# FFN gate and up by token, with seven block products in place of eight for three of eight pairs

## The chip, the core and the metric

One NeuronCore of a Trainium2 chip runs the whole program. Its engines work side by side, each through its own list of instructions: PE (matmul; the profile's PEld is its weight load), DVE (VectorE), ACT (ScalarE), POOL (GpSimd), and SP, which issues most transfers. The metric is the device time of one execution in microseconds, lower is better; the kernel before has a median of 2854.82 us in 3 runs (2853.4 to 2855.13).

## What is computed

One decoder layer on x of 256 tokens and width 2048, in float32: a SwiGLU FFN, a mixer (attention and a state space branch), and a second FFN. The change lies in the two FFNs:

```python
def rms_norm(x, g, eps=RMS_EPS):
    y = xf * lax.rsqrt(jnp.mean(xf * xf, axis=-1, keepdims=True) + eps)
    return (y * g.astype(jnp.float32)).astype(x.dtype)

def swiglu(x, w_gate, w_up, w_down):
    return (jax.nn.silu(x @ w_gate) * (x @ w_up)) @ w_down
...
f = swiglu(rms_norm(h, ffn1_pre_g[i]), ffn1_w_gate[i], ffn1_w_up[i], ffn1_w_down[i])
h = h + 0.5 * rms_norm(f, ffn1_post_g[i])
```

The hidden width is 5632. `w_gate` and `w_up` are 2048 x 5632, `w_down` is 5632 x 2048.

## The kernel before

**Precision.** Each product of two float32 matrices is made of three products of parts: every operand is split into hi (rounded by a copy on ACT) and lo (the rest, a subtraction on DVE), and hi*hi, hi*lo and lo*hi are summed in PSUM. For weights that is `split` (lines 99 to 113): `w_hi` on ACT at L111, `w_lo` on DVE at L112, for 1024 elements of each partition at a time. The pool `wsplit` has 4 buffers of each, so that a split is made when PE has done with the fourth before it. The operand that stays (x, or the hidden values) is split once into a `slot`.

**Weights stream.** Every slab of 1 MB comes through one of three buffers `raw`, by a transfer on SP (L131, L151), and is used once.

**Two forms of projection.** `project` (L121) works by token: x is the operand that PE holds, 128 tokens at a time, and 512 columns of weights move: three matmuls of 512 columns for each 128 rows of weights and each of two token blocks (L117 to L119). `project_t` (L164) works by channel: PE holds 128 x 128 of the weights, and the tokens move, hi and lo of all 256 tokens as 512 columns against `w_hi` (L159), hi alone as 256 columns against `w_lo` (L161). One `project_t` takes 256 output columns through 16 blocks of 128 rows; its result has channels on the partitions.

**FFN.** `ffn` (L290) takes 11 slabs of 512 hidden columns in groups of 4, 4 and 3. For a slab it calls `project_t` four times, gate and up for each half; POOL multiplies gate with the inverse norm of each token before and after the sigmoid function of ACT (L305, L307), DVE multiplies with up (L310), and `fill` splits the result into a slot as it is. After a group, `project` adds the group's part of the down projection to `f`. The norm's factor is spread over partitions once (`spread`), since channels lie on the partitions here.

**Order.** The program is recorded in the order of the code and then put, engine by engine, into an order that the framework's scheduler finds; an engine works through its list strictly. `pre_slots` and `PostNorm` stand between the stages. x and the residual h lie in two buffers of 1 MB (`hpool`).

Of the kernel before, what the change touches and what calls it, by code (L numbers as in the profile page):

```python
# [41 lines left out]
def decoder_layer(ctx: ExitStack, tc: tile.TileContext, x, x_t, cols, rows, post_g, wg1, wu1, wd1, w_in,  # L43
                  w_in_t, w_dt, w_att, w_ssm, w_out, wg2, wu2, wd2, out):
# [10 lines left out]
    acc = E(name="acc", bufs=2, space=bass.MemoryType.PSUM)  # L55
    psm = E(name="psm", bufs=4, space=bass.MemoryType.PSUM)
# [90 lines left out]
    def chunk_t(ps, xs, w, n, c, raw=None, before=None):
        parts = 2 if raw and c == 0 else 1
        if not raw:
            raw = raws.tile([P, 8, 256], F32, name="raw")  # L150
            loaded[0] = nc.sync.dma_start(raw, w(n, c))  # L151
        for b in range(2 * c, 2 * c + 2):
# [614 lines left out]
```

## Time and profile before

| what | value |
|---|---|
| median of 3 runs | 2854.82 us |
| profiled execution, its own time | 2855.79 us |
| its span, first to last instruction | 2853.7 us |
| PE busy | 2814.1 us, 99% |
| DVE busy | 1707.1 us, 60% |
| ACT busy | 1375.2 us, 48% |
| POOL busy | 283.1 us, 10% |
| DMA, mean | 188 GB/s |

The span is cut into stages by their windows: FFN 1 from 7 to 743 us, the mixer to 2103, FFN 2 to 2843. In a row of groups the first number behind the bar is the time in which any of the group was busy, the second the mean of one in ns, and then comes the idle time of its engine just before them, with what ended it. Matmuls overlap, so the time from one start to the next tells their pace.

### The profile page before, as it was taken

What the parts mean: (1) busy time and instruction counts of PE and PEld (TensorE: products, weight loads), DVE (VectorE), ACT (ScalarE), POOL (GpSimd) and SP (SyncE); (2) the same over time, 40 slices, a digit from 0 to 9 for tenths busy, and PEclk for the clock granted to TensorE, in tenths of its full rate; (3) what the DMA queues carried; (4) which work ended last, traced back from release to release, by engine and by line L of the source; (5) the groups of instructions that cost most, each with busy time, mean ns of one, the idle gap of its engine ahead of it and who ended that gap; (6) DMA issues with size and microseconds to landing.
All of it is one profiled execution on the core that took longest, in us unless ns stands there. A gap on an engine that the chain in (4) does not pass through costs nothing.

```text
span 2853.7 us, 36114 instructions
## 1 busy us (share of the span) xinstructions
PE 2814.1 (99%) x14540; PEld 2392.7 (84%) x14540; DVE 1707.1 (60%) x2018; ACT 1375.2 (48%) x1695; POOL 283.1 (10%) x219
## 2 busy tenths in 40 slices
PE   8999999999999999999999999999999999999998
PEld 7888888888788888888788888888878888888887
DVE  6554555555678766777765555545565545555555
ACT  5444444444555555545444444444455444443443
POOL 1100110011013110112100000000001100110110
PEclk9999999999999999999999999999999999999999
DMA  6565555556554555545555545555545555555554
GB/s 240 192 220 190 191 186 190 193 188 205 192 193 168 185 177 176 194 163 192 206 178 176 172 169 183 198 195 187 195 165 189 191 192 192 185 186 195 190 197 155
DMA packets 77127, 537.44 MB, mean 188 GB/s; under 512 B 8672, under 2 KB 8816, under 8 KB 13728
## 3 DMA queue, kind: packets, MB, share of 16 engines
q1 hardware_dynamic: 73152, 521.17, 53.1%
q0 software_dynamic: 3664, 13.80, 1.5%
q8 instruction: 114, 1.87, 0.2%
q14 instruction: 53, 0.43, 0.0%
q10 hardware_dynamic: 144, 0.17, 0.0%
HBM read 530.84 MB, written 4.26 MB: 188 GB/s over the span
## 4 chain that ended last, share of the span: by engine, by line
PE 91%; issue 4%; DVE 3%; ACT 0%; DMA 0%; POOL 0%; SPq 0%; DVEq 0%; POOLq 0%; ACTq 0%
PE acc L159 32%; PE acc L161 16%; PE acc L118 13%; PE acc L119 13%; PE acc L117 13%; DVE w_lo L112 1%; PE pyd L526 1%; PE tp L206 1%; DVE dec L506 1%; PE sc L619 0%; PE po L647 0%; DMA xT<-in_x_t 0%; PE pyo L538 0%; PE pst L533 0%; PE acc_t L119 0%
## 5 line engine op out<-in xcount | busy, mean ns | idle before, releaser
L112 DVE TENSOR_TENSOR w_lo<-raw,w_hi 128x1024 fp32r<-128x1024 f32 (+1 forms) x979 | 1243.9, 1274 | 1026.2 <-ACT w_hi L111 1020.1
L111 ACT ACTIVATE w_hi<-raw 128x1024 fp32r<-128x1024 f32 (+1 forms) x979 | 1034.5, 1059 | 1242.7 <-PE acc L159 619.6
L159 PE MATMUL acc<-slot,w_hi 128*128 128x512 f32 x4096 | 1295.6, 398 | 8.8 <-DVE slot L194 6.9
L161 PEld LDWEIGHTS acc<-slot,w_lo 128*128 128x128 f32 x4096 | 770.1, 188 | 187.8 <-DVE w_lo L112 6.4
L161 PE MATMUL acc<-slot,w_lo 128*128 128x256 f32 x4096 | 807.1, 278 | 4.2 <-DVE w_lo L112 4.2
L118 PE MATMUL acc<-w_lo,slot 128*128 128x512 f32 x1776 | 693.9, 391 | 5.5 <-DVE w_lo L112 5.5
L117 PE MATMUL acc<-w_hi,slot 128*128 128x512 f32 x1776 | 698.0, 393 | 0.0
L119 PE MATMUL acc<-w_hi,slot 128*128 128x512 f32 x1776 | 693.4, 390 | 0.0
L159 PEld LDWEIGHTS acc<-slot,w_hi 128*128 128x128 f32 x4096 | 626.9, 189 | 12.5 <-ACT w_hi L111 9.5
L118 PEld LDWEIGHTS acc<-w_lo,slot 128*128 128x128 f32 x1776 | 334.6, 188 | 76.8 <-DVE w_lo L112 6.5
L117 PEld LDWEIGHTS acc<-w_hi,slot 128*128 128x128 f32 x1776 | 334.6, 188 | 70.3 <-issue 1.2
L119 PEld LDWEIGHTS acc<-w_hi,slot 128*128 128x128 f32 x1776 | 334.4, 188 | 69.3
L305 POOL TENSOR_TENSOR pt<-pt,rb 128x512 f32<-128x512 f32 x44 | 59.9, 1361 | 1110.3 <-DVE pt L177 1105.2
L177 DVE TENSOR_TENSOR pt<-acc,pt 128x512 f32<-128x512 f32 x128 | 87.3, 682 | 1.3 <-ACT pt L176 1.3
L176 ACT ACTIVATE pt<-acc 128x512 f32<-128x512 f32 x128 | 74.3, 580 | 1.2 <-PE acc L161 1.2
L307 POOL TENSOR_TENSOR pt<-pt,rb 128x512 f32<-128x512 f32 x44 | 65.5, 1488 | 32.8 <-ACT pt L306 32.8
L481 DVE SCALAR_TENSOR_TENSOR xc<-pt,col,xc 128x255 f32<-128x255 f32 (+2 forms) x144 | 60.7, 475 | 12.0 <-ACT xc L478 11.9
L513 POOL TENSOR_TENSOR dec<-dec,cb 128x1024 f32<-128x1024 f32 x16 | 54.1, 3394 | 117.7 <-ACT dec L508 117.7
L387 POOL TENSOR_TENSOR pt<-pt,rb 128x512 f32<-128x512 f32 x24 | 34.7, 1447 | 215.7 <-DVE pt L177 154.8
L478 ACT ACTIVATE xc<-pt,col 128x256 f32<-128x256 f32 x48 | 26.9, 595 | 33.8 <-POOL pt L387 33.7
L306 ACT ACTIVATE pt<-pt 128x512 f32<-128x512 f32 x44 | 27.8, 632 | 28.7 <-POOL pt L305 28.7
L310 DVE TENSOR_TENSOR pt<-pt 128x512 f32<-128x512 f32 x44 | 30.5, 692 | 8.8 <-POOL pt L307 4.4
(195 smaller groups left out, 1036.5 us busy)
## 6 DMA issues: line engine op xcount, KB each, us to landing
raw<-in_wu SPq DMA_DIRECT2D x88, 1024.0 KB, 4.9
raw<-in_wd SPq DMA_DIRECT2D x88, 1024.0 KB, 4.9
raw<-in_wg SPq DMA_DIRECT2D x87, 1024.0 KB, 4.9
raw<-in_w_in SPq DMA_DIRECT2D x80, 1024.0 KB, 4.9
raw<-in_w_in_t SPq DMA_DIRECT2D x80, 1024.0 KB, 4.9
raw<-in_w_ssm SPq DMA_DIRECT2D x32, 1024.0 KB, 4.9
raw<-in_w_att SPq DMA_DIRECT2D x16, 1024.0 KB, 4.9
raw<-in_w_out SPq DMA_DIRECT2D x16, 1024.0 KB, 5.0
```

The lines of the kernel that those rows point to most:

```text
L111: nc.scalar.activation(hi[:, js], raw[:, js], AF.Copy)
L112: nc.vector.tensor_tensor(out=lo[:, js], in0=raw[:, js], in1=hi[:, js].bitcast(F32), op=ALU.subtract)
L117: nc.tensor.matmul(ps, xh, wh, start=first, stop=False)
L118: nc.tensor.matmul(ps, xh, wl, start=False, stop=False)
L119: nc.tensor.matmul(ps, xl, wh, start=False, stop=last)
L159: nc.tensor.matmul(ps[:, f], hi[:, j, wf[f]], sl[:, j], start=b + j == 0, stop=False)
L161: nc.tensor.matmul(ps[:, f, TT:], lo[:, j, wf[f]], sl[:, j, :TT], start=False, stop=b == len(xs) - 1 and j == 3)
L176: nc.scalar.activation(out[-1], p[:, :, TT:], AF.Copy)
L177: nc.vector.tensor_tensor(out=out[-1], in0=p[:, :, :TT], in1=out[-1], op=ALU.add)
L305: nc.gpsimd.tensor_tensor(out=g, in0=g, in1=rb, op=ALU.mult)
L307: nc.gpsimd.tensor_tensor(out=g, in0=g, in1=rb, op=ALU.mult)
L481: nc.vector.scalar_tensor_tensor(out=xc[:, j, d:], in0=v[:, k, :TT - d], scalar=w(3 - d), in1=xc[:, j, d:], op0=ALU.mult, op1=ALU.add)
```

## The change

Gate and up go by token, in slabs of 512 hidden columns (11 for each FFN), over 8 pairs of 128-row blocks of the inner width. A transfer of 1 MB now brings a pair's four blocks: gate and up of two row blocks. For five pairs, 8 block products (two token blocks x two row blocks x gate and up) are 24 matmuls. For pairs 2, 4 and 6 (`SP`) seven products take their place, on sums of x's blocks (`sums`, made once in an FFN) and on sums of the weights, which POOL makes from each slab with four additions (`wsum`, L351 to L354) before they are split like weights. Four of the seven (`p1`, `p5`, `p6`, `p7`) have PSUM banks of their own, and are combined on DVE and ACT after the last of the three pairs (L378 to L383); the ordinary pairs are summed in four banks. All 8 banks are then one pool, which the mixer's projections use as well.

The result has tokens on the partitions: the inverse norm becomes a scale for each partition (L390, L392) and POOL has no product there any more, but PE must transpose each slab's result (8 transposes, `to_slot`) before the down projection. Groups are 3, 3, 3 and 2 slabs. The weight sums use the two buffers of `hpool`, so x is read into them late (by POOL's queue, before the last down projection), and the residual of the mixer is written to memory first (`hsave2`).

```diff
+NP = D // (2 * P)
+SP = (2, 4, 6)
+ORDER0 = tuple(range(NP))
+ORDER = (2, 0, 4, 1, 6, 3, 5, 7)
...
-    acc = E(name="acc", bufs=2, space=bass.MemoryType.PSUM)
-    psm = E(name="psm", bufs=4, space=bass.MemoryType.PSUM)
+    psm = E(name="psm", bufs=8, space=bass.MemoryType.PSUM)
...
+            xf = tmp.tile([P, 8, P], F32, name="xf", tag="xc", bufs=2)
+            for f, t, k in ((0, 0, 0), (1, 0, 1), (2, 1, 1), (7, 1, 0)):
+                nc.scalar.activation(xf[:, f], src[:, k, t * P:(t + 1) * P], AF.Copy, scale=g[:, k:k + 1])
+            for f, a, b, op in ((3, 7, 2, ALU.subtract), (4, 3, 0, ALU.subtract), (5, 0, 7, ALU.subtract),
+                                (6, 1, 4, ALU.add)):
+                nc.vector.tensor_tensor(out=xf[:, f], in0=xf[:, a], in1=xf[:, b], op=op)
+            sl = slots.tile([P, 7, 2, P], F32R, name="sums", tag="slot")
+            nc.scalar.activation(sl[:, :, 0], xf[:, :7], AF.Copy)
+            nc.vector.tensor_tensor(out=sl[:, :, 1], in0=xf[:, :7], in1=sl[:, :, 0].bitcast(F32), op=ALU.subtract)
...
+        def prod(k, xh, xl, wh, wl):
+            if k not in bank:
+                bank[k] = psm.tile([P, S], F32, name="gu", tag="m")
+            done[k] += 1
+            nc.tensor.matmul(bank[k], xh, wh, start=done[k] == 1, stop=False)
+            nc.tensor.matmul(bank[k], xh, wl, start=False, stop=False)
+            nc.tensor.matmul(bank[k], xl, wh, start=False, stop=done[k] == count[k])
...
+        for i, p in enumerate(order):
+            raw = fetch(p) if fetch else None
+            if raw is None:
+                raw = raws.tile([P, 4, S], F32, name="raw")
+                nc.sync.dma_start(raw, w[j, p])
+            sl, k0 = xo.at[p]
+            if p in SP:
+
+                e = hpool.tile([P, 4, S], F32, name="wsum", tag="h")
+                nc.gpsimd.tensor_tensor(out=e[:, 0], in0=raw[:, 0], in1=raw[:, 3], op=ALU.add)
+                nc.gpsimd.tensor_tensor(out=e[:, 1], in0=raw[:, 1], in1=raw[:, 3], op=ALU.add)
+                nc.gpsimd.tensor_tensor(out=e[:, 2], in0=e[:, 0], in1=raw[:, 1], op=ALU.add)
+                nc.gpsimd.tensor_tensor(out=e[:, 3], in0=e[:, 2], in1=raw[:, 2], op=ALU.add)
+                ah, al = split(raw[:, 0:2], [P, 2, S])
+                dh, dl = split(raw[:, 2], [P, S])
+                bh, bl = split(e[:, 0:2], [P, 2, S])
+                ch, cl = split(e[:, 2:4], [P, 2, S])
+                x = lambda f: (sl[:, f, 0], sl[:, f, 1])
+                seq = {"p1": (0, ah[:, 0], al[:, 0]), "u0": (6, ah[:, 1], al[:, 1]), "g0": (1, dh, dl),
+                       "p5": (3, bh[:, 0], bl[:, 0]), "p7": (5, bh[:, 1], bl[:, 1]),
+                       "p6": (4, ch[:, 0], cl[:, 0]), "g1": (2, ch[:, 1], cl[:, 1])}
+                for k in (("p1", "p5", "p7", "p6", "u0", "g0", "g1") if i == first else
+                          ("p1", "u0", "g0", "p5", "p7", "p6", "g1")):
+                    f, wh, wl = seq[k]
+                    prod(k, *x(f), wh, wl)
...
+            if i == last:
+                c = {k: new(f"c_{k}") for k in ("g0", "g1", "u0", "u1")}
+                nc.scalar.activation(c["g0"], bank["p1"], AF.Copy)
+                u2 = new("u2")
+                nc.vector.tensor_tensor(out=u2, in0=bank["p6"], in1=c["g0"], op=ALU.add)
+                nc.vector.tensor_tensor(out=c["g1"], in0=bank["p7"], in1=u2, op=ALU.add)
+                nc.vector.tensor_tensor(out=c["u0"], in0=bank["p5"], in1=u2, op=ALU.subtract)
+                nc.vector.tensor_tensor(out=c["u1"], in0=bank["p5"], in1=c["g1"], op=ALU.subtract)
...
+        for t in range(NT):
+            g, u = c[f"g{t}"], c[f"u{t}"]
+            nc.vector.tensor_tensor(out=g, in0=bank[f"g{t}"], in1=g, op=ALU.add)
+            nc.scalar.activation(g, g, AF.Silu, scale=rstd()[:, t:t + 1])
+            nc.vector.tensor_tensor(out=u, in0=bank[f"u{t}"], in1=u, op=ALU.add)
+            nc.vector.scalar_tensor_tensor(out=u, in0=u, scalar=rstd()[:, t:t + 1], in1=g,
+                                           op0=ALU.mult, op1=ALU.mult)
...
+        for a, b in ((0, 3), (3, 6), (6, 9), (9, NFF)):
```

PE, inside a slab of the kernel before: `acc` is the PSUM sum, `slot` is x, `w_hi` and `w_lo` the parts of the weights.

```order
L159 MATMUL acc_1006<-slot_119,w_hi_1029 128x512 x2
L161 MATMUL acc_1006<-slot_119,w_lo_1030 128x256 x2
L159 MATMUL acc_1006<-slot_119,w_hi_1029 128x512 x2
L161 MATMUL acc_1006<-slot_119,w_lo_1030 128x256 x2
L159 MATMUL acc_1006<-slot_119,w_hi_1029 128x512 x2
```

PE, the first pair of the fifth slab of FFN 1 after the change, the first four of its seven products (`gu`: one bank for each; `sums`: x's blocks and their sums).

```order
L335 MATMUL gu_2000<-w_hi_1984,sums_200 128x512
L336 MATMUL gu_2000<-w_lo_1985,sums_200 128x512
L337 MATMUL gu_2000<-w_hi_1984,sums_200 128x512
L335 MATMUL gu_2004<-w_hi_1992,sums_200 128x512
L336 MATMUL gu_2004<-w_lo_1993,sums_200 128x512
L337 MATMUL gu_2004<-w_hi_1992,sums_200 128x512
L335 MATMUL gu_2008<-w_hi_1992,sums_200 128x512
L336 MATMUL gu_2008<-w_lo_1993,sums_200 128x512
L337 MATMUL gu_2008<-w_hi_1992,sums_200 128x512
L335 MATMUL gu_2012<-w_hi_1996,sums_200 128x512
L336 MATMUL gu_2012<-w_lo_1997,sums_200 128x512
L337 MATMUL gu_2012<-w_hi_1996,sums_200 128x512
```

Every matmul now has 512 columns, three for one product; seven products make 21 matmuls for a pair, and PE changes its bank after each three.

DVE, where two slabs meet, before: the last sum of a projection (`pt<-acc`), its product and its split into a slot stand singly among the splits.

```order
L112 TENSOR_TENSOR w_lo_616<-raw_593,w_hi_615 128x1024
L177 TENSOR_TENSOR pt_543<-acc_458,pt_543 128x512
L310 TENSOR_TENSOR pt_543<-pt_543,pt_452 128x512
L112 TENSOR_TENSOR w_lo_645<-raw_642,w_hi_644 128x1024
L187 TENSOR_TENSOR slot_122<-pt_543,slot_122 128x2x256
L112 TENSOR_TENSOR w_lo_665<-raw_642,w_hi_664 128x1024
```

DVE after the change, where the fourth slab of FFN 1 (`c_..._185x`) meets the fifth, whose first pair comes through `raw_1977` and `wsum_1979`, the second through `raw_2028`.

```order
L121 TENSOR_TENSOR w_lo_1993<-wsum_1979,w_hi_1992 128x1024
L121 TENSOR_TENSOR w_lo_2075<-raw_2063,w_hi_2074 128x512
L389 TENSOR_TENSOR c_g0_1857<-gu_1692,c_g0_1857 128x512
L121 TENSOR_TENSOR w_lo_1997<-wsum_1979,w_hi_1996 128x1024
L391 TENSOR_TENSOR c_u0_1859<-gu_1688,c_u0_1859 128x512
L389 TENSOR_TENSOR c_g1_1858<-gu_1696,c_g1_1858 128x512
L392 SCALAR_TENSOR_TENSOR c_u0_1859<-c_u0_1859,pre_rstd_510,c_g0_1857 128x512
L391 TENSOR_TENSOR c_u1_1860<-gu_1719,c_u1_1860 128x512
L121 TENSOR_TENSOR w_lo_2031<-raw_2028,w_hi_2030 128x1024
L392 SCALAR_TENSOR_TENSOR c_u1_1860<-c_u1_1860,pre_rstd_510,c_g1_1858 128x512
L121 TENSOR_TENSOR w_lo_2035<-raw_2028,w_hi_2034 128x1024
```

The six operations that end a slab stand together, with one split of the next slab's first pair behind the first of them, and the second pair's splits behind the fifth and the sixth.

## Rows read from the trace of the kernel before

**Rows 1.** The page: span, busy time of each engine, chain that ended last.

```profile
span 2853.7 us, 36114 instructions
...
PE 2814.1 (99%) x14540; PEld 2392.7 (84%) x14540; DVE 1707.1 (60%) x2018; ACT 1375.2 (48%) x1695; POOL 283.1 (10%) x219
...
PE 91%; issue 4%; DVE 3%; ACT 0%; DMA 0%; POOL 0%; SPq 0%; DVEq 0%; POOLq 0%; ACTq 0%
```

**Rows 2.** Windows of one `project_t` pair each, FFN 1: length, busy us by engine, clock, DMA.

```profile
core 0: us, PE busy (x) PEld busy (x) DVE busy (x) ACT busy (x) POOL busy (x), PEclk, DMA share, GB/s
49.36:71.66 22.30, 22.30 (x130) 19.46 (x129) 12.56 (x12) 10.68 (x13) 2.79 (x3) 1.00 0.56 190
71.66:93.95 22.29, 22.29 (x130) 19.45 (x129) 12.62 (x12) 10.61 (x13) 2.78 (x3) 1.00 0.55 189
```

**Rows 3.** Timeline of PE, last down projection of FFN 1: start, us, what.

```profile
729.80 0.39 PE L117 MATMUL acc_t<-w_hi,slot 128*128 128x512 f32 x1
...
742.49 0.40 PE L119 MATMUL acc_t<-w_hi,slot 128*128 128x512 f32 x1
```

**Rows 4.** Timeline of PE in the mixer: eight transposes.

```profile
977.11 1.03 PE L206 MATMUL tp<-ident,y 128*128 128x128 f32 x8
977.98 0.82 PE L496 MATMUL px<-ident,xc 128*128 128x128 f32 x6
```

**Rows 5.** Groups in two windows of rows 2; below, two single forms (groups, timeline).

```profile
L112 DVE TENSOR_TENSOR w_lo<-raw,w_hi 128x1024 fp32r<-128x1024 f32 x16 | 20.2, 1262 | 19.2 <-ACT w_hi L111 19.2
L111 ACT ACTIVATE w_hi<-raw 128x1024 fp32r<-128x1024 f32 x17 | 18.0, 1060 | 23.5 <-PE acc L159 22.3 <-issue 1.2
L305 POOL TENSOR_TENSOR pt<-pt,rb 128x512 f32<-128x512 f32 x3 | 3.9, 1292 | 43.6 <-DVE pt L177 43.6
L177 DVE TENSOR_TENSOR pt<-acc,pt 128x512 f32<-128x512 f32 x4 | 2.7, 682 | 0.0
...
L283 DVE SCALAR_TENSOR_TENSOR hb<-f,post_r,hb 128x512 f32<-128x512 f32 x12 | 8.4, 747 | 2.7 <-POOL post_r L275 2.7
...
6.83 0.69 DVE L112 TENSOR_TENSOR w_lo<-raw,w_hi 128x512 fp32r<-128x512 f32 x1
```

**Rows 6.** Timelines of DVE and POOL, 48 to 51 us: a split meets a product.

```profile
47.46 1.23 DVE L112 TENSOR_TENSOR w_lo<-raw,w_hi 128x1024 fp32r<-128x1024 f32 x1 [0.56 <-ACT w_hi L111]
50.24 1.50 DVE L112 TENSOR_TENSOR w_lo<-raw,w_hi 128x1024 fp32r<-128x1024 f32 x1 [0.95 <-ACT w_hi L111]
...
49.36 1.29 POOL L305 TENSOR_TENSOR pt<-pt,rb 128x512 f32<-128x512 f32 x1 [6.06 <-DVE pt L177]
```

**Rows 7.** Timelines: two splits alone (19 us); two beside two POOL additions (741 us).

```profile
19.02 2.35 DVE L112 TENSOR_TENSOR w_lo<-raw,w_hi 128x1024 fp32r<-128x1024 f32 x2
...
741.14 4.52 DVE L112 TENSOR_TENSOR w_lo<-raw,w_hi 128x1024 fp32r<-128x1024 f32 x2
...
740.63 3.94 POOL L282 TENSOR_TENSOR h<-h,f 128x512 f32<-128x512 f32 x2 [0.87 <-ACT f L281]
```

**Rows 8.** Timelines, 881 us: DVE operations that read PSUM beside a POOL product.

```profile
881.25 1.28 DVE L529 TENSOR_TENSOR y<-pyd,xv 128x512 f32<-128x512 f32 x2
...
881.48 1.29 POOL L387 TENSOR_TENSOR pt<-pt,rb 128x512 f32<-128x512 f32 x1 [9.31 <-DVE pt L177]
```

**Rows 9.** Timelines of DVE, POOL and PE, 985 to 993 us, mixer.

```profile
986.34 2.59 DVE L520 TENSOR_TENSOR xdd<-xv,dend 128x512 f32<-128x512 f32 x1
988.85 4.49 DVE L112 TENSOR_TENSOR w_lo<-raw,w_hi 128x1024 fp32r<-128x1024 f32 x2
...
985.97 5.16 POOL L513 TENSOR_TENSOR dec<-dec,cb 128x1024 f32<-128x1024 f32 x2 [18.70 <-ACT dec L508]
...
992.26 0.50 PE L161 MATMUL acc<-slot,w_lo 128*128 128x256 f32 x2 [3.62 <-DVE w_lo L112]
```

**Rows 10.** Groups by form: gains, small sums and squares on DVE.

```profile
L194 DVE SCALAR_TENSOR_TENSOR slot<-xT,col,slot 128x256 fp32r<-128x256 f32 x16 | 6.7, 480 | 1.9 <-ACT slot L193 1.8
...
L512 DVE TENSOR_TENSOR cb<-pcb,tri 128x128 f32<-128x128 f32 x16 | 4.2, 281 | 0.0
...
L345 DVE TENSOR_TENSOR sq<-sq 128x1024 f32<-128x1024 f32 x3 | 3.7, 1218 | 0.7 <-ACT sq L343 0.7
```

**Rows 11.** Windows: the start of FFN 1, and the mixer.

```profile
7.00:29.00 22.00, 19.56 (x98) 15.63 (x99) 18.52 (x28) 18.26 (x30) 0.00 (x0) 1.00 0.87 342
...
751.00:2103.00 1352.00, 1340.27 (x6735) 1130.15 (x6734) 867.05 (x1195) 671.15 (x879) 137.39 (x99) 0.99 0.54 184
```

**Rows 12.** DMA issues: KB each, us to landing.

```profile
raw<-in_wu SPq DMA_DIRECT2D x88, 1024.0 KB, 4.9
...
hsave<-h SPq DMA_DIRECT2D x2, 1024.0 KB, 4.2
```

More of the change, by code (lines that the diff above doesn't have):

```diff
@@ L100, in split @@
     def split(raw, shape, parts=1, before=None):
-        hi = wsplit.tile(shape, F32R, name="w_hi", tag="whi")
-        lo = wsplit.tile(shape, F32R, name="w_lo", tag="wlo")
+        one = shape[1:] == [S]
+        hi, lo = (wsplit.tile(shape, F32R, name=f"w_{p}", tag=f"w{p}{'1' if one else ''}", bufs=2 if one else None)
+                  for p in ("hi", "lo"))
         k = shape[1] // parts
@@ L143, in project, with project_t @@
             for sl_, j, wh, wl, first, last in tail:
-                matmul3(at(t), sl_, j, t, wh, wl, first, last)
+                matmul3(ps[t], sl_, j, t, wh, wl, first, last)
         return ps
[L147 to L152, printed above, removed]
-            hi, lo = split(raw[:, 4 * (b % 2):4 * (b % 2) + 4], [P, 4, 256], parts if b == 0 else 1,
-                           before and (lambda js: before(b, js)))
+    def project_t(xs, w, n):
+        ps = [psm.tile([P, 2 * TT], F32, name="acc", tag="m") for _ in range(2)]
+        for b in range(len(xs)):
+            if b % 2 == 0:
+                raw = raws.tile([P, 8, 256], F32, name="raw")
+                nc.sync.dma_start(raw, w(n, b // 2))
+            hi, lo = split(raw[:, 4 * (b % 2):4 * (b % 2) + 4], [P, 4, 256])
             sl = xs[b].rearrange("p j i t -> p j (i t)")
@@ L312, in ffn, with final @@
             if not post:
-                if first:
-                    with tc.issue_after(loaded[0].ins):
-                        for t in range(NT):
-                            nc.sync.dma_start(h[t], x[t * P:(t + 1) * P])
                 post = PostNorm(gi, 0.5)
                 f = post.f
+            def final():
+                flush()
+                return hs[-1]
+            lazy = hs + [final]
             for n in range(4):
-                last = b == NFF
-                pd = project(hs, lambda n, c: wd[n, a + c], n, by_token=2 if last and n == 3 else 0)
+                pd = project(lazy, lambda n, c: wd[n, a + c], n, by_token=2 if last and n == 3 else 0)
@@ L322, in ffn @@
                 part = f[:, :, n * S:(n + 1) * S]
-                if a == 0:
-                    nc.scalar.activation(part, pd, AF.Copy)
-                elif not last:
-                    nc.vector.tensor_tensor(out=part, in0=pd, in1=part, op=ALU.add)
+                if not last:
+                    for t in range(NT):
+                        if a == 0:
+                            nc.scalar.activation(part[:, t], pd[t], AF.Copy)
+                        else:
+                            nc.vector.tensor_tensor(out=part[:, t], in0=pd[t], in1=part[:, t], op=ALU.add)
@@ L333, in ffn @@
         return post.finish()
-    xs = [new_slot() for _ in range(4)]
+    x1 = pair_slots()
     def scale1():
```

201 lines of the change are left out of this document (126 added, 75 removed).

## Prediction

> **What bounds the kernel now.** I read the page's shares first: PE is busy 99% of a span of 2853.7 us, DVE 60%, ACT 48%, POOL 10%, and 91% of the chain that ended last is PE [rows 1]. The windows say that this holds in each stage that the change touches: two `project_t` of the first FFN fill 22.30 us without a gap, and in them DVE is busy 12.6 us, ACT 10.6, POOL 2.8, at the full granted clock [rows 2]. In such a stretch only the number and the pace of matmuls set the time. The reader should take two paces from it. `project_t` spends 22.30 us on 2 x 16 groups of four matmuls (two of 512 columns, two of 256), so 0.697 us a group. `project`, whose matmuls all have 512 columns, goes from start 729.80 to start 742.49 in 56 steps, so 0.2266 us each [rows 3]. The mean of one in a list of groups is no pace, as neighbours overlap.
>
> **The change, part by part.** A slab is 512 columns of the hidden width; there are 11 in each FFN, 22 in all. All sums are against the profiled execution, 2855.8 us, which is 1.0 above the median of 2854.8.
>
> *Matmuls of gate and up.* Before, a slab is four `project_t`: 2 x 22.30 = 44.60 us. After, it is 8 pairs of blocks; five take 24 matmuls of 512 columns, three take 21: 183 x 0.2266 = 41.47 us. By token without the scheme it would be 192 x 0.2266 = 43.51. So the form gains 1.09 and the scheme 2.04.
>
> The Trainium skill, "TensorE: Matmul & The Clock Gate", section "Back-to-back issue gap", gives columns/2.4 + 2.5 ns for an isolated matmul. By it both forms run at almost one speed per column, a slab's matmuls would go from 41.6 to 39.5 us, and with the transposes 22 slabs would gain 27 us. The trace does not agree: both paces are longer in it, and both forms run in this kernel, so the rows decide and the rule gets no chance of its own.
>
> *Transposes.* The token form gives gate times up with tokens on the partitions, so each slab needs 8 transposes by PE. A row of eight starts at 977.11 and its successor at 977.98: 0.87 us [rows 4]. A slab of PE work is then 41.47 + 0.87 = 42.34 us, 2.26 less than before; 22 x 2.26 = **49.7 us less** if PE never waits.
>
> *DVE.* A slab needs 19 `w_lo` of 1024 at 1.22 us, 3 of 512 at 0.69, ten operations of 512 that read PSUM (four combinations, four last sums, two fills) at 0.68, and two products at 0.75 [rows 5]: 23.2 + 2.1 + 6.8 + 1.5 = 33.6 us. Before it was 2 x 12.6 = 25.2. So DVE goes from 57% to 79% of a slab. ACT gets 19 `w_hi` at 1.06 and some 5 us besides, 25 us, and stays off the path.
>
> *POOL and DVE together.* POOL loses two products of each half slab and gets 12 additions of 512 elements a slab; at the 1.29 of its present product [rows 5] they take 15.5 us. These fit into 42 us, but they disturb DVE. A `w_lo` that meets a POOL addition takes 1.50 us instead of 1.23 [rows 6]. Two `w_lo` beside two POOL additions take 4.52 us, where two alone take 2.35, and the two additions take 3.94 [rows 7]. One waits for the other: the full price is 1.08 us of DVE per addition. Two DVE operations that read PSUM are not disturbed: 1.28 us beside a POOL operation that keeps its 1.29 [rows 8]. That a late DVE stops PE is in the trace as well: beside two large POOL products one `xdd` takes 2.59 us, two `w_lo` 4.49, and PE stands 3.62 us for a `w_lo` [rows 9].
>
> The Trainium skill, "SBUF — State Buffer", section "Who interferes with whom", says that a DVE instruction with two SBUF inputs and a GpSimd one that reads SBUF exclude each other for a whole instruction, and speaks against this use of POOL; by that rule, the trace agrees.
>
> So DVE has 33.6 us a slab plus 12 times something between 0.3 (the row where DVE had gaps) and 1.08 (where it had none): 37 to 46.6 us against 42.34 of PE. I take a value nearer the first, some 0.6, since DVE still has gaps in which POOL can work, and ten PSUM operations beside which it works free: 40.8 us. DVE is then nearly full and no longer far ahead.
>
> *The border of two slabs.* There the order of DVE puts six operations that end a slab among the splits of the next. The first of them waits for the `g0` sum, whose last matmul is 9 matmuls (2.04 us) ahead of the slab's end. Behind it stand the split of the first pair's last sums, `u0`, `g1`, one product, `u1`, and the first `w_lo` of the second pair: 0.68 + 1.22 + 0.68 + 0.68 + 0.75 + 0.68 + 1.22 = 5.9 us, so that this `w_lo` is done 3.9 us after the border. PE asks for it after the first pair's 21 matmuls, 4.76 us. That is 0.9 us in hand without POOL; two full collisions cost 2.2 and make it 1.3 late. I take **0.5 us of waiting a slab, 11 us** (bounds 0 and 1.3 x 22 = 29).
>
> *The two starts.* No row shows the first slab of an FFN in the new form. In it DVE also builds the operands: ten gains at 0.48, three sets of four small subtractions (0.28 each) and one of 896 elements (about 1.1), and in FFN 1 the squares (3 x 1.22 + 1.1): 16 us [rows 10]. With the 33.6 this is 50 against 42.3, and already now PE is busy only 19.56 of the first 22 us there [rows 11]. I take 8 us for FFN 1 (bounds 0 and 15). In FFN 2 the first sum must also wait until the residual has been written out, as it takes the same buffers: landing 4.2 us [rows 12], four additions, a split. Two ordinary pairs (10.9 us) cover most of it; I take 5 (bounds 0 and 10). **13 us** together.
>
> *At nothing:* the down projections (same matmuls; four groups for three add 0.68 us sums on DVE, which idles there), the larger ring of PSUM banks in the mixer, the copy of x read later by POOL's queue (the last down projections, 192 matmuls or 43 us, cover it). If the ring delays a bank in the mixer, PE waits at places like those of [rows 9].
>
> Sum: 2855.8 - 49.7 + 11 + 13 = 2830.1 profiled, **2829 us** for the median.
>
> **Rivals.**
>
> *No wait at all.* DVE's gaps swallow the additions and the starts cost what they do now: 2855.8 - 49.7 + 3 = 2809. For it: DVE now waits for ACT 19 us of 44.6 [rows 5]; against it: the 4 to 6 us bunch at each border.
>
> *DVE and POOL become the bound (slower).* With 1.08 us per addition DVE needs 46.6 us a slab, 2.0 more than the 44.6 of now: 2855.8 + 44 + 13 = 2913. It decides from 0.73 us per addition (33.6 + 12 x 0.73 = 42.3, where PE starts to wait), and the kernel loses from 0.92. For it: additions come four in a row and DVE, once behind, always has work, as in [rows 7]. Against it: ten operations of DVE read PSUM, and the gaps.
>
> *The weight slab is held too long.* Three buffers, one slab needed every 5.3 us: 15.9 us to go round. A slab of the scheme is held for landing 4.9 [rows 12], four additions (5.2 alone, 7.9 at the pace of [rows 7]) and a split of 2.3: 12.4 to 15.1. It fits by 0.8 us at worst. If the fixed order of DVE holds it longer by 1.6, each of 66 such pairs loses 0.75 us, which is all of the gain: 2855.8 + 13 = 2869.
>
> *The change does little.* The mixer, whose order of instructions also changes, takes back what FFN gains: 2855.
>
> **How the numbers follow.** Forecast 0.42, no wait 0.24, DVE and POOL 0.16, slab held 0.12, little 0.06. A measurement of this kernel tells 0.2% (5.7 us) from no change. Faster: 0.24 and nearly all of 0.42, so 0.65; same: 0.06 and the edge of the forecast, 0.08; slower: 0.27. The range goes from the sum without any wait and a little more (2803) to past the held slab (2890); that leaves out the full collision above and some 4 in 100 below.
>
> **What would show it.** Right: a slab of gate and up takes 42.5 to 43.5 us, DVE is busy some 40 us of it, `w_lo` has a mean of 1.4 to 1.6 us, PE's idle time there ends with `w_lo`, about 0.5 us a slab, most of it just after a border; POOL's additions take 1.3 to 2 us. Wrong: a slab at 44.6 or more with DVE without gaps (collision), or PE waiting for a `w_hi` that waits for a transfer (slab held), or a pace of the new matmuls other than 0.2266, or a mixer longer than its 1352 us [rows 11] by more than 5.

## Result and profile after

The changed kernel takes 2879.8 us (median of 4 runs, 2878.3 to 2880.8) against 2855.0 of the kernel before: a ratio of 1.0086, 95% interval 1.0068 to 1.0103. It is **slower by 25 us**; 2829 had been forecast.

The page of after, span and busy time, to be held against [rows 1]:

```profile
span 2878.2 us, 33689 instructions
...
PE 2788.6 (97%) x13102; PEld 2314.0 (80%) x13102; DVE 2073.4 (72%) x2321; ACT 1452.9 (50%) x1830; POOL 661.6 (23%) x401
```

PE is busy 25.5 us less and the span is 24.5 us longer: PE now stands still. To see where, I cut every trace at four instructions of PE: the first matmul, the first transpose of FFN 1's result (`h`), the first transpose of the mixer's (`hb`), and the last matmul. "Group" is a steady group of FFN 1: three slabs of gate and up and their down projection, from start to start (before: groups of four, 265.4 us, which is 199.05 for three slabs). The stages are those of the profiled execution, the median that of all; in e1 and e9 the profiled one was 7 us below the median.

| kernel (us) | FFN 1 | mixer | FFN 2 | first group | group | median |
|---|---|---|---|---|---|---|
| before | 735.9 | 1361.2 | 740.6 | | 199.05 | 2855 |
| after | 740.9 | 1379.3 | 741.6 | 217.7 | 196.1 | 2879.8 |
| e1 ring alone | 741.0 | 1376.6 | 750.0 | | | 2892.3 |
| e2 conv first | 740.2 | 1373.8 | 741.4 | 217.1 | 196.3 | 2872.2 |
| e3 no additions | 717.1 | 1380.1 | 717.1 | 202.8 | 192.8 | 2832.4 |
| e4 additions unused | 738.7 | 1379.0 | 744.6 | 217.1 | 194.9 | 2878.3 |
| e5 form alone | 735.8 | 1381.9 | 739.5 | 205.2 | 198.95 | 2873.3 |
| e6 mixer banks | 744.9 | 1360.5 | 734.1 | 218.5 | 195.8 | 2857.2 |
| e7 additions on DVE | 724.9 | 1379.2 | 720.1 | 210.4 | 192.9 | 2842.4 |
| e8 squares by token | 751.7 | 1379.7 | 740.6 | 228.1 | 196.5 | 2887.9 |
| e9 two and two | 760.8 | 1374.9 | 761.4 | 215.7 | 204.7 | 2921.7 |
| e10 DVE and banks | 727.0 | 1361.3 | 720.1 | 208.5 | 192.9 | 2825.8 |
| e11 with squares late | 726.3 | 1360.7 | 717.3 | 208.2 | 192.9 | **2822.7** |
| e12 with squares early | 730.3 | 1360.7 | 717.4 | 211.6 | 192.9 | 2825.3 |
| e13 additions elsewhere | 848.3 | 1379.9 | 854.1 | 334.0 | 192.8 | 3100.5 |
| e14 two and two, no wait | 764.1 | 1380.0 | 761.2 | 217.7 | 204.5 | 2922.7 |
| e15 additions of hi | 740.9 | 1378.5 | 738.7 | 217.7 | 196.5 | 2878.8 |

So the FFNs, where 26 us were to be won, lose 5.1 and 1.0, and the mixer, which was to stay as it was, loses 18.1. Two places of the trace of after show how. The first is the mixer's start, on PE's timeline. Before, 111 matmuls of a projection stand between these two rows:

```profile
785.77 0.33 PE L407 MATMUL pdv<-ident,dtT 64*128 64x64 f32 x2
...
806.38 0.49 PE L434 MATMUL pcs<-da,tri 128*128 128x128 f32 x2 [0.79 <-DVE da L432]
```

After:

```profile
790.81 0.45 PE L519 MATMUL pdv<-ident,dtT 64*128 64x64 f32 x2 [3.18 <-DVE dtT L516]
799.91 0.77 PE L546 MATMUL pcs<-da,tri 128*128 128x128 f32 x2 [8.65 <-DVE da L544]
800.47 0.53 PE L550 MATMUL ptot<-da,ones 128*128 128x64 f32 x2
800.92 1.12 PE L558 MATMUL pat<-tri,da 128*64 128x128 f32 x4
801.97 0.59 PE L571 MATMUL plam<-lam,ones 128*128 128x2 f32 x2
802.42 1.20 PE L167 MATMUL acc<-slot,w_hi 128*128 128x512 f32 x2
```

PE waits 8.65 us for `da`, the end of a chain of some 25 small DVE operations on dt, though the next matmuls of `project_t` (L167) need nothing of it. And the two windows behind it (length, busy us by engine, granted clock, DMA) show a second price: after the standstill the granted clock is at its lower level, 0.50.

```profile
799.90:806.50 6.60, 6.59 (x23) 5.57 (x24) 1.09 (x4) 0.69 (x3) 1.13 (x2) 0.50 0.05 10
806.50:812.00 5.50, 5.50 (x32) 4.77 (x32) 2.05 (x2) 2.12 (x2) 0.00 (x0) 0.98 0.00 0
```

Over the whole mixer PE's 6753 matmuls keep it busy 1344.3 us before and 1347.2 after: of the 18.1 us, 2.9 are slower work and 15.2 are waits.

The second place is the border of two slabs in FFN 1; timelines of DVE, of POOL, and PE's two waits:

```profile
266.70 1.29 DVE L121 TENSOR_TENSOR w_lo<-raw,w_hi 128x512 fp32r<-128x512 f32 x1 [2.19 <-ACT w_hi L120]
267.91 0.68 DVE L389 TENSOR_TENSOR c_g<-gu,c_g 128x512 f32<-128x512 f32 x1
268.51 1.71 DVE L121 TENSOR_TENSOR w_lo<-wsum,w_hi 128x1024 fp32r<-128x1024 f32 x1
...
272.61 1.72 DVE L121 TENSOR_TENSOR w_lo<-raw,w_hi 128x1024 fp32r<-128x1024 f32 x1
...
267.40 1.75 POOL L352 TENSOR_TENSOR wsum<-raw 128x512 f32<-128x512 f32 x1
269.11 2.27 POOL L353 TENSOR_TENSOR wsum<-wsum,raw 128x512 f32<-128x512 f32 x1
...
270.28 0.50 PE L336 MATMUL gu<-w_lo,sums 128*128 128x512 f32 x1 [0.83 <-DVE w_lo L121]
274.39 0.50 PE L336 MATMUL gu<-w_lo,slot 128*128 128x512 f32 x1 [1.09 <-DVE w_lo L121]
```

The small split at 266.70 takes 1.29 us instead of 0.69, the two of 1024 take 1.71 and 1.72 instead of 1.22, and the additions beside them 1.75 and 2.27 instead of 1.29: that is the meeting of [rows 7], in the bunch of operations that ends a slab. `c_g`, which reads PSUM, keeps its 0.68 beside an addition, as in [rows 8]. The loss falls mostly on the first border of a group, where the additions come in the same microseconds: the two waits shown, 1.9 us, are all that the list of PE's waits has in the group that starts at 225.2 us. Counted from start to start PE loses 2.5 us at this border, of the 3.3 by which the group is longer than the same group without additions (e3, below).

### The profile page after: what moved, and what is told of

It reads as the page before. It is cut to its first block, busy times and chain, and to the rows that moved or that the text cites. A ratio compares the mean times of both kernels' runs of the same rounds, so it can differ in the third digit from the quotient of the medians.

```text
span 2878.2 us, 33689 instructions
## 1 busy us (share of the span) xinstructions
PE 2788.6 (97%) x13102; PEld 2314.0 (80%) x13102; DVE 2073.4 (72%) x2321; ACT 1452.9 (50%) x1830; POOL 661.6 (23%) x401
## 5 line engine op out<-in xcount | busy, mean ns | idle before, releaser
L167 PE MATMUL acc<-slot,w_hi 128*128 128x512 f32 x1280 | 409.6, 401 | 0.1
L336 PE MATMUL gu<-w_lo,slot 128*128 128x512 f32 x880 | 347.1, 394 | 17.1 <-DVE w_lo L121 16.8
L335 PE MATMUL gu<-w_hi,slot 128*128 128x512 f32 x880 | 344.6, 392 | 7.5 <-ACT w_hi L120 7.5
L337 PE MATMUL gu<-w_hi,slot 128*128 128x512 f32 x880 | 344.1, 391 | 0.0
L351 POOL TENSOR_TENSOR wsum<-raw 128x512 f32<-128x512 f32 x66 | 105.4, 1596 | 836.7 <-DMA raw<-in_wgu 811.5
L169 PEld LDWEIGHTS acc<-slot,w_lo 128*128 128x128 f32 x1280 | 241.9, 189 | 61.5 <-DVE w_lo L121 4.5
L169 PE MATMUL acc<-slot,w_lo 128*128 128x256 f32 x1280 | 253.5, 279 | 3.8 <-DVE w_lo L121 3.8
L336 PEld LDWEIGHTS gu<-w_lo,slot 128*128 128x128 f32 x880 | 166.2, 189 | 62.5 <-DVE w_lo L121 28.5
L167 PEld LDWEIGHTS acc<-slot,w_hi 128*128 128x128 f32 x1280 | 197.9, 190 | 3.3 <-issue 2.8
L335 PEld LDWEIGHTS gu<-w_hi,slot 128*128 128x128 f32 x880 | 165.8, 189 | 41.8 <-ACT w_hi L120 7.5
L336 PE MATMUL gu<-w_lo,sums 128*128 128x512 f32 x462 | 182.7, 396 | 13.3 <-DVE w_lo L121 13.3
L121 DVE TENSOR_TENSOR w_lo<-wsum,w_hi 128x1024 fp32r<-128x1024 f32 x132 | 180.6, 1382 | 17.9 <-ACT w_hi L120 17.6
L337 PEld LDWEIGHTS gu<-w_hi,slot 128*128 128x128 f32 x880 | 166.1, 189 | 33.7
```

What stands on the lines that cost most here:

```text
L121: nc.vector.tensor_tensor(out=lo[:, js], in0=raw[:, js], in1=hi[:, js].bitcast(F32), op=ALU.subtract)
L167: nc.tensor.matmul(ps[f], hi[:, j, wf[f]], sl[:, j], start=b + j == 0, stop=False)
L169: nc.tensor.matmul(ps[f][:, TT:], lo[:, j, wf[f]], sl[:, j, :TT], start=False, stop=b == len(xs) - 1 and j == 3)
L335: nc.tensor.matmul(bank[k], xh, wh, start=done[k] == 1, stop=False)
L336: nc.tensor.matmul(bank[k], xh, wl, start=False, stop=False)
L337: nc.tensor.matmul(bank[k], xl, wh, start=False, stop=done[k] == count[k])
```

## The experiments

Theory A: the mixer loses by the ring of PSUM banks. Banks of one ring are given in the order in which the code asks. The first conv projection asks for its two after `pcs`, `ptot`, `pat` and `plam`, so PE's order puts it behind them; before, projections had a pool of their own. Theory C1: in the FFNs, DVE and POOL disturb each other at the memory port that they share. Its rivals: the splits wait for the additions (C2), DVE's fixed order and late transfers would make the same waits without POOL (D), or POOL holds the weight slabs too long (H, from the prediction).

**e1, the ring alone**, in the kernel before (`project`, `project_t` and the readers of their results as in the changed kernel):

```diff
-    acc = E(name="acc", bufs=2, space=bass.MemoryType.PSUM)
-    psm = E(name="psm", bufs=4, space=bass.MemoryType.PSUM)
+    psm = E(name="psm", bufs=8, space=bass.MemoryType.PSUM)
...
```

> The kernel before, with one edit: all PSUM banks in one ring of 8, as in the changed kernel; the FFNs keep project_t. Theory A (the ring gives banks in the order of the program, so the first conv projection must stand behind pcs, ptot, pat and plam, and PE waits for DVE's chain on dt): 2866 to 2873 us against 2855, the mixer's time from the first transpose of FFN 1's result to the first hb transpose grows from 1361 to 1372 to 1379 us, and two gaps of 3 and 9 us stand round pdv and pcs. Rival B (the mixer is longer because of what the FFN leaves behind, the clock or the buffers of h): 2853 to 2858 us.

2892.3 us, ratio 1.0126 (1.0111 to 1.0141). The mixer behaves as A says: 1376.6 us, and PE waits 3.18 us ahead of `pdv` and 8.65 ahead of `pcs`, as in after. The total was missed, as the FFNs lose too (5.1 and 9.4): with `project_t` the ring puts `spread`'s small matmuls ahead of the next projection, and PE waits for them, 2.70 us in FFN 1 and 7.93 in FFN 2:

```profile
2165.24 1.20 PE L242 MATMUL rb<-pre_diag,ones 128*128 128x128 f32 x4 [7.93 <-DVE pre_diag L241]
```

The changed kernel has no `spread` in its FFNs, so these waits are not part of its loss.

**e2, conv first**, in the changed kernel:

```diff
...
+    bct0 = conv_silu([T_BC, T_BC + 1], [32, 33, 40, 41])
     pcs = psm.tile([P, NT, 64], F32, name="pcs", tag="m")
```

> The changed kernel, with the first conv projection recorded ahead of pcs, so that it gets its banks first. Theory A: the gap of 8.85 us ahead of pcs goes, and with it a stretch at the lower clock; 2865 to 2870 us against 2880, the mixer 1365 to 1370 us. Rival B: 2877 to 2881 us, since the same chain on DVE would then stop another instruction.

2872.2 us, 1.0056 (1.0040 to 1.0073). The gap ahead of `pcs` is gone, but the mixer falls only by 5.4, to 1373.8: less than expected. The gap ahead of `pdv` stayed (`pdv` still asks first), and so did smaller ones further on. The order round `pcs` is one part of the loss; whether the ring makes the rest had to be asked for the whole mixer.

**e6, the mixer's banks as before:** PSUM is one ring of 8 in each FFN, and divided as before between them: `banks(True)` gives two double tiles and four banks, `banks(False)` the ring of eight.

```diff
...
+    banks(True)
     xs = pre_slots(C_MIX, update)
...
+    banks(False)
     update, x2 = post.finish(), pair_slots()
```

> The changed kernel, with PSUM divided in the mixer as before (two double tiles for the projections, four banks for the rest) and one ring of eight in the FFNs only. Theory A (all that the mixer lost comes from the ring): the mixer falls from 1379 to 1361 to 1364 us, the total to 2860 to 2865 us. Rival B2 (the ring explains the order round pcs alone, the rest of the loss is the clock's or the FFN's): mixer 1370 or more, total 2869 to 2873 us.

2857.2 us, 1.0004 (0.9995 to 1.0014): 22.6 us less than the changed kernel, and the mixer is at 1360.5, as before. All of the mixer's loss is the ring's. The mixer alone gives back 18.8 us of the 22.6; FFN 1 became 4.0 longer and FFN 2 7.5 shorter, which was not followed up. In e6 the conv projection runs ahead of `pcs`, and the wait has shrunk to 0.65 us:

```profile
809.49 0.28 PE L188 MATMUL acc<-slot,w_lo 128*128 128x256 f32 x1
810.41 0.46 PE L566 MATMUL pcs<-da,tri 128*128 128x128 f32 x2 [0.65 <-DVE da L564]
```

**e3, no additions, and e4, additions that nobody reads.** e3 drops the four lines L351 to L354 (their part of the computation is left out); e4 keeps them. In both the products read raw blocks:

```diff
...
-                bh, bl = split(e[:, 0:2], [P, 2, S])
-                ch, cl = split(e[:, 2:4], [P, 2, S])
+                bh, bl = split(raw[:, 0:2], [P, 2, S])
+                ch, cl = split(raw[:, 2:4], [P, 2, S])
```

> The changed kernel without POOL's four additions: blocks of the raw slab are split in their place (part of the computation is left out; matmuls, splits and transfers are as many as before). Theory C (waits in FFN come from the additions, by the port or by their chain): w_lo of 1024 goes back to 1.25 us, the steady group of three slabs with its down projection falls from 196.0 to 193 to 194 us, the first groups by 5 to 10 us more; 2850 to 2862 us. Rival D (waits come from the order of DVE at a border and from the transfer that comes late): group 195.5 to 196, total 2872 to 2880 us.

> As the run without additions, but POOL still makes the four additions into the same buffers, and nobody reads them (the products use raw blocks). If the port is the cause (C1), w_lo stays at 1.40 us and the steady group at 195.5 to 196.5 us, total 2872 to 2882 us. If the cause is that splits must wait for the additions (C2), the group falls as without them, 193 to 194 us, total 2850 to 2864 us.

2832.4 us (0.9919, 0.9905 to 0.9934) and 2878.3 (1.0081, 1.0066 to 1.0096). The 47 us between e3 and the changed kernel come back to within 2 when POOL adds for nobody. The orders of PE, DVE and ACT are the same in both, row by row. So no split's wait for an addition matters (C2 falls), and neither do order and transfers by themselves (D falls): it is the additions' presence. The groups over the same three slabs, 225.2 to 354.7 us, show it; first after:

```profile
L121 DVE TENSOR_TENSOR w_lo<-raw,w_hi 128x1024 fp32r<-128x1024 f32 x41 | 65.2, 1614 | 7.1 <-ACT w_hi L120 7.1
L353 POOL TENSOR_TENSOR wsum<-wsum,raw 128x512 f32<-128x512 f32 x8 | 17.1, 2143 | 0.0
```

then e3:

```profile
L121 DVE TENSOR_TENSOR w_lo<-raw,w_hi 128x1024 fp32r<-128x1024 f32 x56 | 67.8, 1222 | 35.3 <-ACT w_hi L120 34.9
```

and e4:

```profile
L121 DVE TENSOR_TENSOR w_lo<-raw,w_hi 128x1024 fp32r<-128x1024 f32 x58 | 87.3, 1542 | 9.2 <-ACT w_hi L120 9.2
```

A split has a mean of 1.61, 1.22 and 1.54 us. What kind of operation is hit can be counted in FFN 1 of after: the 101 splits of 1024 columns that run beside an addition have a mean of 1.94 us (longest 2.38), the 197 others 1.22. DVE's sums that read PSUM have 0.68 in either case, and ACT's `w_hi` has 1.06 in after as in e3. So not everything that touches the memory becomes slower: operations of DVE with both inputs in SBUF do. The Trainium skill, "SBUF — State Buffer", section "Who interferes with whom", calls the port that the two engines share an exclusive lock. The traces agree: in e4 nothing passes from POOL to DVE and both are slowed, and no split beside an addition took longer than the two alone, 1.22 + 1.29 us.

**e13 and e15, the port without the hold.** In e4 POOL still reads the raw slabs, and so keeps them from the next transfer. e13 lets POOL add blocks of x's slots, one copy on ACT pacing it; e15 lets it add the two halves of `w_hi`, which ACT has just made:

```diff
+                for a in range(4):
+                    nc.gpsimd.tensor_tensor(out=e[:, a], in0=ah[:, 0].bitcast(F32), in1=ah[:, 1].bitcast(F32), op=ALU.add)
```

> As the run with unused additions, but POOL adds blocks of the x slots, so that it neither waits for a weight slab nor holds one (part of the computation is left out; one copy of a single column on ACT paces POOL). In the run with unused additions POOL still held the slabs. Theory C1 (the shared port): the time stays near 2878: 2868 to 2884 us, w_lo of 1024 in the steady groups at 1.45 to 1.65 us, group 194.5 to 196.5. Rival H (the slab is held too long by POOL, and the next transfer is late): as without additions, 2830 to 2850 us, group near 193, though w_lo stays long.

> As the run with unused additions, with the same orders on PE and DVE, but POOL's four additions read w_hi of the pair (in SBUF, just made by ACT) and not the raw slab, so that POOL no longer holds a slab and no order has to be paced by ACT (part of the computation is left out). The run before this one failed to tell the two causes apart, since POOL made all its additions at once. Theory C1 (the shared port): 2868 to 2884 us, group 194.5 to 197. Rival H (POOL holds the slab, the next transfer is late): 2830 to 2850 us, group near 193.

e13, 3100.5 us (1.0856, 1.0838 to 1.0874), missed its aim: the pacing copy was put ahead of the splits in ACT's order, POOL made all 132 additions of an FFN in the first group (334 us), and ACT stood waiting for them. The later groups, without any, are at 192.8. As a total it decides nothing, but its trace shows the meeting without any hold of a slab: in FFN 1 the 27 splits of 1024 beside an addition of x's blocks have a mean of 2.12 us, the 271 others 1.23. e15 tells C1 and H apart: 2878.8 us (1.0084, 1.0067 to 1.0101), group 196.5, as in the changed kernel, with the slabs free and the orders of PE, DVE and ACT those of e4. H falls; **POOL's additions beside DVE's splits are the cause of the FFNs' loss.** That they meet at the shared port rests on the kind of operations that are hit, and on the section of the Trainium skill named above. One reserve on the size in e15: POOL now holds `w_hi`, and ACT waits 5.7 us for that in the window of three slabs. Splits have a mean of 1.70 us there:

```profile
L121 DVE TENSOR_TENSOR w_lo<-raw,w_hi 128x1024 fp32r<-128x1024 f32 x58 | 96.7, 1700 | 8.3 <-ACT w_hi L120 8.0
L354 POOL TENSOR_TENSOR wsum<-w_hi 128x512 f32<-128x512 f32 x33 | 66.5, 2044 | 44.8 <-ACT w_hi L120 44.8
```

**e5, the form alone:** all pairs by token, no scheme.

```diff
-SP = (2, 4, 6)
+SP = ()
...
```

> The changed kernel without the scheme: all eight pairs take 24 matmuls by token, no sums of x or of weights, no combinations. Theory C1 (every wait in FFN comes from the port that DVE and POOL share): without additions nothing waits, a slab is 192 x 0.2266 + 0.87 = 44.4 us, which is the run without additions (2832.4) plus 22 x 2.04 = 45: 2870 to 2880 us, the steady group of three slabs 198 to 199.5 us. So the scheme's three products saved would be just what its additions cost. Rival E (the token form has waits of its own at the borders of slabs): 2884 us or more.

2873.3 us, 1.0058 (1.0043 to 1.0073), group 198.95: as C1 has it, and as long as before (199.05), so the form alone gains nothing. The scheme saves 6.2 us of a group of three slabs when nothing disturbs it (198.95 to 192.8 in e3), and the additions and the first slabs take it all back: e5 and the changed kernel are 6 us apart, in e5's favour.

**e7, additions on DVE:**

```diff
-                nc.gpsimd.tensor_tensor(out=e[:, 0], in0=raw[:, 0], in1=raw[:, 3], op=ALU.add)
-                nc.gpsimd.tensor_tensor(out=e[:, 1], in0=raw[:, 1], in1=raw[:, 3], op=ALU.add)
-                nc.gpsimd.tensor_tensor(out=e[:, 2], in0=e[:, 0], in1=raw[:, 1], op=ALU.add)
-                nc.gpsimd.tensor_tensor(out=e[:, 3], in0=e[:, 2], in1=raw[:, 2], op=ALU.add)
+                nc.vector.tensor_tensor(out=e[:, 0:2], in0=raw[:, 0:2], in1=raw[:, 3:4].broadcast_to([P, 2, S]), op=ALU.add)
+                nc.vector.tensor_tensor(out=e[:, 2], in0=e[:, 0], in1=raw[:, 1], op=ALU.add)
+                nc.vector.tensor_tensor(out=e[:, 3], in0=e[:, 2], in1=raw[:, 2], op=ALU.add)
```

> The changed kernel with the additions on DVE (one of 1024 and two of 512 for each pair, some 2.6 us), POOL idle. Theory C1 (the time of the shared port counts: 19 w_lo, 3 small ones, two products and 12 additions are 42.3 us of it a slab, against 42.3 of PE): the port falls to 34.5 and DVE to some 41.3 us a slab; steady group 193 to 195.5 us, total 2858 to 2872 us. Rival F (DVE in its fixed order is the bound, whoever adds): steady group 196 or more, total 2876 to 2890 us.

2842.4 us, 0.9948 (0.9931 to 0.9964): better than the range given. POOL's additions, moved to the engine that was late, make that engine *less* busy. The same window, after and e7 (columns as in [rows 2]):

```profile
225.20:354.70 129.50, 127.48 (x566) 104.33 (x565) 114.66 (x95) 70.76 (x78) 58.42 (x31) 1.00 0.53 191
```

```profile
225.20:354.70 129.50, 129.50 (x581) 107.20 (x579) 108.73 (x119) 71.28 (x77) 0.00 (x0) 1.00 0.56 202
```

DVE goes from 114.7 to 108.7 us, and PE has no gap left.

**e9, two additions on POOL, two on DVE** (the first two as in the changed kernel, the others as in e7):

> The changed kernel with the first two additions of a pair on POOL and the other two on DVE. Theory C1 (time of the shared port): 26.8 + 6 x 1.29 + 6 x 0.69 = 38.7 us of the port a slab, 3.6 less than with four on POOL and 4 more than with none; steady group 193 to 194.5 us, total 2846 to 2860 us, between the run with additions on DVE (2842.4) and the changed kernel (2879.8). Rival F2 (any addition on POOL brings the waits, as splits wait for it): group 195.5 or more, total 2870 or more.

2921.7 us, 1.0239 (1.0221 to 1.0257): 42 us slower than the changed kernel, with a group of 204.7. That is far outside C1's numbers and inside F2's. The time of the port does not account for it: splits are back at 1.24 us and DVE is busy 103 of the 129.5 us of that window. DVE's timeline at a border shows another wait:

```profile
266.79 1.76 DVE L354 TENSOR_TENSOR wsum<-wsum,raw 128x512 f32<-128x512 f32 x1 [3.13 <-POOL wsum L352]
268.47 0.68 DVE L121 TENSOR_TENSOR w_lo<-raw,w_hi 128x512 fp32r<-128x512 f32 x1
269.07 0.68 DVE L390 TENSOR_TENSOR c_g<-gu,c_g 128x512 f32<-128x512 f32 x1
```

DVE's third addition waits for POOL's two, POOL for a transfer, and behind it in DVE's fixed order stand the sums that end the slab (`c_g`). I took that wait for the cause (theory J) and tried it.

**e14**, as e9, but the third addition reads raw blocks alone:

```diff
-                nc.vector.tensor_tensor(out=e[:, 2], in0=e[:, 0], in1=raw[:, 1], op=ALU.add)
+                nc.vector.tensor_tensor(out=e[:, 2], in0=raw[:, 0], in1=raw[:, 1], op=ALU.add)
```

> As the run with two additions on POOL and two on DVE, but DVE's third addition reads two raw blocks, not POOL's result (part of the computation is changed), so that DVE doesn't wait for POOL there. If that wait was the cause of 2921.7 us (theory J), 2845 to 2862 us and a group of 193 to 195 us, as first expected of that run by the time of the port. Rival K (the halves on two engines cost by their transfers or by ACT's order, since the split of POOL's sums still waits for it): 2900 us or more.

2922.7 us (1.0231, 1.0216 to 1.0247), so J falls; the number is in K's range, but nothing else was run on K. The same place in e14:

```profile
266.12 0.69 DVE L354 TENSOR_TENSOR wsum<-raw 128x512 f32<-128x512 f32 x1 [1.33 <-DMA raw<-in_wgu]
266.79 1.73 DVE L121 TENSOR_TENSOR w_lo<-raw,w_hi 128x512 fp32r<-128x512 f32 x1
268.44 1.77 DVE L355 TENSOR_TENSOR wsum<-wsum,raw 128x512 f32<-128x512 f32 x1
270.14 0.68 DVE L390 TENSOR_TENSOR c_g<-gu,c_g 128x512 f32<-128x512 f32 x1
```

Now DVE waits for the transfer itself, and two small operations that meet POOL's additions (1.73 and 1.77 us for 0.69) stand ahead of `c_g`. That DVE's order puts a later slab's work ahead of the sums could explain both kernels; it was not tried. The cause of these two runs stays open, and with it how far "time of the port" can be used as a measure: it forecast e7 too slow and e9 too fast.

**e8, squares by token:** FFN 1's squares on ACT from a copy of x by token, instead of ACT, DVE and two matmuls.

```diff
+                nc.gpsimd.dma_start(xr, x[t * P:(t + 1) * P, c * S:(c + 1) * S])
+                nc.scalar.activation(junk, xr, AF.Square, accum_out=ss[:, t, c:c + 1])
```

> The changed kernel, with the squares of FFN 1 summed by ACT from a copy of x by token (as in the other norms) in place of ACT, five DVE additions and two matmuls. Theory C1: the first slab has 16 us of further DVE work on the port, 4.8 of it goes, and the wait of 2.5 us ahead of the sums' matmul too; first group 217.7 to 209 to 213 us, total 2871 to 2876 us. Rival G (the first slab waits for transfers or for ACT): 2878 to 2882 us.

2887.9 us, 1.0110 (1.0095 to 1.0125): 8 us worse, not better. The waits of e8 between 40 and 130 us (total, times, longest) and POOL's timeline point to a cause: the loads of x stand behind POOL's additions, and ACT's `w_hi` behind the squares.

```profile
ACT junk L457 <- DMA xr<-in_x: 17.2, 4, 10.9
DVE w_lo L121 <- ACT w_hi L120: 17.1, 6, 8.1
```

```profile
87.97 2.14 POOL L354 TENSOR_TENSOR wsum<-wsum,raw 128x512 f32<-128x512 f32 x1
90.06 1.61 POOL L455 DMA_DIRECT2D xr<-in_x  x3
```

**e10 to e12, the repairs together:** e6 and e7 in one kernel; in e11 and e12 the squares by token as well, since POOL's queue is now empty, recorded after the last or the fourth pair.

> Both repairs together: additions on DVE, PSUM divided in the mixer as before. If the two causes are independent, 2842.4 - 22.6 = 2820 us (2815 to 2824), faster than both kernels; if they share time (the clock, a stall that hides the other), 2825 to 2835.

> As the run with both repairs, and the squares by token, recorded at the end of the first slab. POOL's queue now holds no additions, so the eight transfers of x go out at once. If the harm in the earlier run with squares by token came from transfers that stood behind POOL's additions (ACT waited 10.9 us for one), the 6.6 us wait ahead of the sums' matmul goes and nothing takes its place: 6 to 9 us less than the run with both repairs. Rival: ACT's order or the t2 buffers are the cause, and it is 5 us or more slower than that run.

> As the run before, with the squares recorded after the fourth pair. Same as that run within 3 us if only the transfers' place on POOL's queue mattered.

2825.8 us (0.9893, 0.9878 to 0.9908), 2822.7 (0.9883, 0.9869 to 0.9898) and 2825.3 (0.9892, 0.9877 to 0.9907). The two repairs together give 54 us where the sum of the two alone is 60, just inside the second range of the expectation. The mixer's part is there in full (17.9 us from e7 to e10, 18.8 from the changed kernel to e6). What is missing is FFN 2: it became 7.5 us shorter in e6, where POOL still adds, and is the same in e10 as in e7.

In e11 and e12 the squares by token do no harm, which fits the transfers' place on POOL's queue as the cause in e8. What they gain, 3 us and nothing, is below what was expected: in e11 PE's wait of 6.5 us ahead of the sums' matmul goes, but its waits for `w_hi` and `w_lo` in FFN 1's first group grow from 8.8 to 13.5. FFN 1, the only stage that the edit touches, is 0.7 us shorter than in e10 in e11, and 3.3 longer in e12. e11 is the fastest: **33 us faster than before, 57 faster than the change.**

## Why the prediction was wrong

The forecast of 2830.1 was missed by 49.9 us in the profiled execution. 31.8 of these are in the FFNs and 18.1 in the mixer, and it took both to turn a gain into a loss: with the FFNs as forecast the ring alone would have left some 2848 (2830.1 + 18.1, an estimate), and with the mixer repaired e6 is at 2857, no change.

**The first step that failed** is the term "At nothing: ... the larger ring of PSUM banks in the mixer", for which no reason was given. It measured +18.1 us (e6 gives them back). The prediction had named the right sign to look for, a mixer longer by more than 5, but looked for it at the places of [rows 9], where PE's wait has not changed (3.63 us). The harm sits where four small matmuls at the end of a DVE chain ask for banks ahead of a large projection. The order of PE in the two kernels shows this ahead of any run: before, 111 matmuls of a projection stand between `pdv` and `pcs`; now none do.

**The second, and larger, is the size of the waits in the FFNs**: named rightly, and taken at half. The sum had 11 us at the borders and 13 at the two starts, 24. The additions alone cost 23.8 us in FFN 1 and 24.5 in FFN 2 (after against e3), 48. And e3's FFNs are 42.2 us below those of before where its steady pace alone would give 45.8; the other 3.6 are put down to the starts here.
- The price of an addition was right: DVE's busy time in the window of three slabs is 114.7 us, and 92.0 in e3; 22.6 us for the 31 additions that lie in it or the 36 of three slabs is 0.73 or 0.63 each, where 0.6 was taken. (The split alone is 1.22 us in e3, as taken; [rows 5], named for it, has 1.26.)
- The border was not: 196.1 - 192.8 is 1.1 us a slab, 24 for 22, where 0.5 was taken and 1.3 was the bound. It is not spread evenly: at the first border of a group three splits of the bunch are hit and PE waits 0.83 and 1.09 us; the other borders cost little.
- The first slabs were not. FFN 1's first group is 14.9 us longer than in e3 and FFN 2's 13.6 (206.7 against 193.1); if the three borders in each cost 3.3 as above, the additions cost the starts 11.6 and 10.3. With e3's 3.6 that is 25.5, an estimate, where 8 + 5 was taken and 15 + 10 was the bound. In the first slab DVE is busy 55.5 of 58.7 us, and PE 48.5:

```profile
7.50:66.20 58.70, 48.49 (x188) 36.79 (x188) 55.45 (x58) 36.88 (x55) 32.93 (x17) 0.94 0.56 208
```

**PE's work was nearly right.** Without disturbance three slabs take 192.8 us instead of 199.05, 2.08 us a slab against 2.26 in the sum: -45.8 in place of -49.7. The scheme gave what was forecast (6.15 us of three slabs from e5 to e3, 3 x 2.04 in the sum). The form did not: 1.09 less 0.87 for transposes was to leave 0.22 a slab, and e5 shows 0.03.

**The rivals.** "DVE and POOL become the bound" did not come about in the steady slabs (DVE is busy 89% of their time), but describes the first slab. "The weight slab is held too long" fell with e15. "No wait at all", 2809, is near what e3 and the mixer's repair together would give: 2832.4 - 22.6 = 2810 with e6's gain, 2816 with the 16.6 from e7 to e10. That is an estimate, as the two were not run together. "The mixer takes back what FFN gains" had 0.06; it did, with the FFNs' gain already gone.

**What the profile was to show:** a slab of 42.5 to 43.5 us (129.5 / 3 = 43.2, yes), `w_lo` at 1.4 to 1.6 us (1.40 and 1.61), additions at 1.3 to 2 us (1.60 for the first of the four, 2.1 for the third), PE's waits ended by `w_lo` after a border (yes, twice as long, and mostly after the first of a group). The range reached to 2890, so 2879.8 lies in it by its width; that is no merit of the mechanism.

## What to carry to other kernels

Count an edit of a shared resource in every stage that uses it, not only in the stage it was made for: two pools of PSUM that become one ring tie together the orders of matmuls that had been free of each other, and the scheduled order of PE shows it without any run. Work handed to an idle engine that shares a port with the critical one is not free; sum both engines' time at the port, above all in the bunch with the least in hand, and ask whether the critical engine could do the work itself (here 0.6 to 0.7 us for 512 columns on DVE against 1.6 to 2.1 on POOL). And a total is no forecast: DVE was less busy in e9 than in the changed kernel, and e9 was the slower by 42 us, for a reason that its sums do not show.

## What was not expected of the hardware

POOL's addition of 512 elements, 1.29 us alone, once took 6.59 us in the changed kernel (at 53.5 us, in the first slab, where DVE has hardly a gap), 6.91 in e8 (at 40.8) and 7.33 in e15 (at 29.8): a dense stretch of DVE held POOL up for five times the addition's own duration. DVE's splits in FFN 1 never took more than 2.38 us beside additions, less than double their 1.22.

And PE's standstill here cost more than its length: after the 8.65 us ahead of `pcs` the granted clock was at 0.50, the level of 1.2 GHz, for the 6.6 us in which PE was busy again. It had fallen earlier, in the wait ahead of `pdv`: the 9.9 us from 790.0 are at 0.50 too.
